# V as one level of Strassen, half swaps on ScalarE, and a new order of residuals and weights in the feed-forward, in a decoder layer on eight cores

## The chip, the cores and the metric

One Trainium2 chip, all 8 cores: two dies (cores 0 to 3 and 4 to 7), and four pairs of neighbours (0/1, 2/3, 4/5, 6/7). Each core computes 2048 of the 16384 tokens, and K and V also of the 2048 tokens before its own. The metric is the device time of the slowest core in microseconds (us). TensorE is called PE here, VectorE DVE, ScalarE ACT, GpSimd POOL, SyncE SP. The fast runs of one kernel can agree closely, but some executions fall into a slower state in which a die is granted a lower clock (a run of `b_same` took 3204.8 us with cores 0 to 3 at 0.863 to 0.873 and cores 4 to 7 at 0.990 to 0.992); only fast runs are compared below. A ratio is the mean time of one kernel's fast runs over that of the other's of the same rounds, so it is not quite the ratio of the medians that are quoted.

## The reference, cut to what matters

```python
proj = x @ w_in + b_in          # Q, K, V of two groups of heads
# group A: 8 heads of 128, three dilated windows; group B: 16 query heads of 64 on 2 K/V heads, window 128
# both: rotary positions on q and k; RMSNorm per group; concatenation -> w_out
x = layer_norm(alpha * x + mixer(x))
x = layer_norm(alpha * x + swiglu(x))      # D_MODEL 2048, D_FF 5632
```

The stages of a core follow each other: V and K (tiles of 512 tokens, 8 tiles), queries and attention, out-projection with the first LayerNorm, feed-forward in four groups (two strips of tokens, st, by two halves of the hidden units, g), the last LayerNorm.

## The kernel before

The feed-forward is already Strassen; V is plain. For tile t and block blk of 128 tokens, V is 16 products a bank, and rope of a K head is four DVE instructions:

```python
def v_tile(t, blk):                      # before
    groups = [(0, 512), (512, 1024)] if (t < 4 and not (t == 3 and blk == 3)) else [(0, 384), (384, 768), (768, 1152)]
    ...
            for kc in range(KC):         # KC = 16
                nc.tensor.matmul(bank(k, bk)[:, 0:c1 - c0], x[:, kc, blk * 128:blk * 128 + 128], wv[:, kc, c0:c1], ...)

# rope_a: t2[0:64]   = (ps[64:128] + bias) * sin      DVE
#         t2[64:128] = (ps[0:64]  + bias) * sin       DVE
#         t1         = (ps + bias) * cos              DVE
#         dst        = t1 + t2                        DVE, fp32 in, bf16 out

# ra: two rope tables, loaded two tiles ahead; KO: three buffers from which K heads are stored

for t in range(2, 8):                    # before, shortened
    if t >= 3: kb_tile(t)
    for blk in range(4): v_tile(t, blk)
    if t == 7: phase2_loads(k)           # what attention needs first
    for h in range(8): k_tile(t, h)      # each ends in a store from KO, issued by SP
    if t + 2 < 8: load_ra(t + 2)
```

`phase2_loads` issues on SP, among others, one load that reads what V's stores have written, and so waits for all of them:

```python
S_.dma("sp", k.vB, k.vs_d[TOK - 128:2 * TOK, 1024:1152]..., k.bvs, [k.bvB], "vB")
```

In the feed-forward each group is 22 up steps (`fl`, a 1 MB weight tile each, three places) and 8 down pairs (`p`, a 1.4 MB weight tile each, three places that overlap those of the up tiles). The residual rows of a down pair (`xq`) are loaded one pair ahead, the results stored to z2s:

```python
U_OFF = [WB, WB + 8192, WB + 16384]                                          # up step i uses U_OFF[i % 3]
D_OFF = [WB + (24576, 13312, 0)[i] for i in (0, 1, 2, 0, 1, 2, 1, 0)]        # place of the weights of down pair p
...
for p in range(5 if last else KC // 2):
    nxq = load_xq(p + 1) if p < 7 else None
    ...
    P("5", BB, True, True, cs);  P("2", BC, True, True, cs)
    acc(q11, BB, ALU.subtract, True);  acc(q22, BB, ALU.subtract, True)      # DVE: needs the residuals
    if p: d_sums(st, g, p, "R")                                              # DVE: needs the weights of pair p
    P("4", BA, True, True, cs);  acc(q21, BC, ALU.add, True)
    if p < 7: d_sums(st, g, p + 1, "P")                                      # DVE: needs the weights of pair p + 1
    ...
    if st == 0 and g == 1 and 1 <= p <= 4: load_x1((B11, B22, B12, B21)[p - 1])
```

The softmax here doesn't subtract the row's maximum and nothing guards it: scores larger than these inputs give would overflow.

Of the kernel before, what the change touches and what calls it, by code (L numbers as in the profile page):

```python
# [18 lines left out]
KC = D // 128  # L19
# [293 lines left out]
def persist(k):  # L313
# [12 lines left out]
    k.p_end = P.o  # L326
# [9 lines left out]
XO = 4096  # L336
X_SLOT = 16384


def rope_a(k, bk, ch, cs, sn, brope, t1, bt1, t2, bt2, dst, bdst, order=None, later=None):  # L340
# [18 lines left out]
    if later is None:  # L359
        for f in (f1, f2, f3, f4):  # L360
            f()
    else:
        later += [f1, f2, f3, f4]


def rope_b(k, bk, ch, n, cs, sn, brope, pre, bpre, t1, bt1, t2, bt2, dst, bdst, later):
# [4 lines left out]

    def tail():
        S_.pe(lambda: nc.tensor.matmul(ps, k.perm, pre[:, 0:n], start=True, stop=True), [bpre, k.bperm], [k.bBK[bk]])
        S_.dve(lambda: nc.vector.tensor_tensor(out=t1[:, 0:n], in0=pre[:, 0:n], in1=cs, op=ALU.mult), [bpre, brope], [bt1])
        S_.dve(lambda: nc.vector.tensor_tensor(out=t2[:, 0:n], in0=ps, in1=sn, op=ALU.mult), [k.bBK[bk], brope], [bt2])  # L375
        S_.dve(lambda: nc.vector.tensor_tensor(out=dst, in0=t1[:, 0:n], in1=t2[:, 0:n], op=ALU.add), [bt1, bt2], [bdst])
    later.append(tail)


def phase1(k):  # L380
    nc, S_ = k.nc, k.S
    xs = [view(k, XO + i * X_SLOT, KC * 512).rearrange("p (a b) -> p a b", a=KC) for i in range(5)]
    P = Place(k, XO + 5 * X_SLOT, 2 * ARENA_EL)
    wv, _ = P("wv", KC * VW)
    o = XO + 5 * X_SLOT
# [9 lines left out]
    ra, bra, rb, brb = [], [], [], []  # L395
    for i in range(2):
        v, b = P("ra%d" % i, 1024, F32)
        ra.append(v.rearrange("p (a b) -> p a b", a=2))
        bra.append(b)
    v, b = P("rb", 1024, F32)  # L400
    rbt, brbt = v.rearrange("p (a b) -> p a b", a=2), b
    bv, bbv = P("bv", VW, F32)
    T1 = [P("t1%d" % i, 512, F32) for i in range(2)]
    T2 = [P("t2%d" % i, 512, F32) for i in range(2)]
    PRE = P("pre", 512)
    KO = [P("ko%d" % i, 512) for i in range(3)]
    VO = [P("vo%d" % i, VW) for i in range(2)]
# [7 lines left out]
    slot_of = [0, 1, 2, 4, 0, 1, 2, 3]  # L415
# [55 lines left out]
    def v_tile(t, blk):  # L471
        x = xs[slot_of[t]]
        groups = [(0, 512), (512, 1024)] if (t < 4 and not (t == 3 and blk == 3)) else [(0, 384), (384, 768), (768, 1152)]
        banks = []
        for (c0, c1) in groups:
            bk = nx("bk", 8)
            banks.append(bk)

            def mm(bk=bk, c0=c0, c1=c1):
                for kc in range(KC):  # L480
                    ins = nc.tensor.matmul(bank(k, bk)[:, 0:c1 - c0], x[:, kc, blk * 128:blk * 128 + 128], wv[:, kc, c0:c1],  # L481
                                           start=(kc == 0), stop=(kc == KC - 1))
                return ins
            S_.pe(mm, bx[t] + bwv + ([bwvb] if c1 > 1024 else []), [k.bBK[bk]])
        v_out(t, blk, groups, banks)

    def k_tile(t, h):
        x = xs[slot_of[t]]
        bk = nx("bk", 8)
        ri = t % 2  # L490
# [8 lines left out]
        ko, bko = KO[ki := nx("ko", 3)]  # L499
        rope_a(k, bk, h, ra[ri][:, 0, :], ra[ri][:, 1, :], bra[ri], T1[ti][0], T1[ti][1], T2[ti][0], T2[ti][1], ko, bko)  # L500
# [4 lines left out]
    def kb_tile(t):  # L505
# [12 lines left out]
        ki = nx("ko", 3)  # L518
        ko, bko = KO[ki]
        rope_b(k, bk, 8, n, rbt[:, 0, 0:n], rbt[:, 1, 0:n], brbt, PRE[0], PRE[1], T1[ti][0], T1[ti][1], T2[ti][0], T2[ti][1],  # L520
# [8 lines left out]
    def load_ra(t):  # L529
        S_.dma("sp", ra[t % 2], k.ropeA_d[t], [], [bra[t % 2]], "ra%d" % (t % 2))  # L530
# [25 lines left out]
    load_ra(1)  # L556
    for h in range(8):
        k_tile(0, h)
    load_x(2, (8, 8))
    load_ra(2)  # L560
    for h in range(8):
        k_tile(1, h)
        if h == 0:
            load_x(3, (8, 8))
    load_ra(3)
    S_.dma("sp", rbt[:, :, 0:128], k.ropeBh_d, [], [brbt], "rb")
    for t in range(2, 8):
        if t == 2:
            load_x(4, (8, 8))
            load_x(5, (8, 8))  # L570
        if t == 3:
            load_x(6, (8, 8))
            load_x(7, (8, 8))
        if t >= 3:
            kb_tile(t)
        for blk in range(4):
            v_tile(t, blk)
            flush()
        if t == 7:
            k.xs, k.bx = xs, bx  # L580
            phase2_loads(k)
        if 3 <= t < 7:
            S_.dma("sp", rbt, k.ropeB_d[t - 3], [], [brbt], "rb")
        for h in range(8):
            k_tile(t, h)
        if t + 2 < 8:
            load_ra(t + 2)
    flush()
# [35 lines left out]
def phase2(k):  # L624
# [93 lines left out]
    peq = []  # L718

# [8 lines left out]
    def proj(tau, bk=None, mid=None):  # L728
# [21 lines left out]
        if ci < 8:  # L750
            pre, bpre = PRE[ti]
            rope_b(k, bk, 17 + ci, 512, rb[:, tt, 0], rb[:, tt, 1], brb, pre, bpre, T1[ti][0], T1[ti][1], T2[ti][0],
                   T2[ti][1], q[:, tt * 512:(tt + 1) * 512], bq[tt], peq)
# [149 lines left out]
    def a_banks(u):  # L903
        return (6, 7) if u >= 26 and u % 2 else (OB, LB)
# [109 lines left out]
    for tau in range(LEAD):  # L1014
        proj(tau, (6, 7, 4, 5)[tau % 4])
        if tau:
            run(peq, 1)
        if tau == LEAD - 2:
            pend = b_S(0, 0)
    for u in range(32):  # L1020
        j, kq = u // 4, u % 4
        nxt = b_S((u + 1) // 4, (u + 1) % 4) if u < 31 else None
        if u == 31:
            spend = [a_S(0, 0, 2, 0), a_S(0, 0, 1, 1)]
        b_PV(j, kq, pend)
        b_evac(j, kq)
        proj(u + LEAD, mid=lambda: run(peq, 1))
        run(dveq, 4)
        if u == 3:
# [9 lines left out]
    for u in range(32):  # L1039
# [5 lines left out]
        for p_ in range(3):  # L1045
# [4 lines left out]
            if p_ == 0:  # L1050
                run(dveq, 2 if u < 26 else 4)
# [36 lines left out]
D_OFF = [WB + (24576, 13312, 0)[i] for i in (0, 1, 2, 0, 1, 2, 1, 0)]  # L1088
# [44 lines left out]
def out_loads(k):  # L1133
# [5 lines left out]
    for st in range(2):  # L1139
        for g in range(2):  # L1140
            if st == 0 and g == 0:
                k.wlist.append(("gate", st, g))
            k.wlist += [(("u", st, f), k.wup_d[f].rearrange("q p n -> p q n"), KC * 256, KC, BF16, U_OFF[f % FG % 3]) for f in range(g * FG, (g + 1) * FG)]
# [6 lines left out]
    for c in KCB + KCA[:7]:  # L1150
        y_load(k, 1, c)

# [59 lines left out]
def phase3(k):  # L1212
# [112 lines left out]
    def load_x1(b):  # L1325
# [656 lines left out]
```

## Time and profile before

| | before |
|---|---|
| time, median of 3 runs | 2954.8 us (2952.95; the third, 3379.08, was slow) |
| span of the profiled execution, slowest core | 2858.0 us, granted clock 0.990 |
| PE busy in it | 2754.1 us (96%) |
| V and K, first to last K product | 417.4 us |
| feed-forward, first to last product start (eight cores) | 1640.7 to 1655.5 us |

A line of the time line reads: start, duration, engine, line of the program, operation, output and input with their shape, how many; in brackets the idle time just before and what ended it. Lines of the kernel before and after have different numbers. Those that are needed: feed-forward products L1399 before, L1505 after; accumulations L1745 before, L1861 after; K products L494 before, L590 after; V units L528 after; query projections L742 before, L836 after.

### The profile page before, as it was taken

Reading aid. Unit: us, or ns where it says so; the run is one execution under the profiler, and the core shown is the slowest. Engines: PE = TensorE matmul, PEld = TensorE weight load, DVE = VectorE, ACT = ScalarE, POOL = GpSimd, SP = SyncE. Lnnn points to the kernel's source line nnn. Section 1 sums busy time; section 2 is a strip of 40 time slices with the busy share of each in tenths; the row PEclk is TensorE's granted clock in tenths of the full one; section 3 lists DMA queues with packets and bytes.
Section 4 is the critical chain, followed back from the end, with each engine's and each line's share of the span. In section 5 each row is a group of like instructions: output and inputs, shape, how many; then the busy total and the mean of one; then the engine's idle time right before and its main releaser. Section 6 shows DMA issues by size and latency. Waiting matters only on the chain.

```text
span 2858.0 us, 41512 instructions; the slowest of 8 cores (2846.2 to 2858.0 us)
## 1 busy us (share of the span) xinstructions
PE 2754.1 (96%) x15081; PEld 1319.9 (46%) x15081; DVE 1933.6 (68%) x2707; ACT 736.6 (26%) x1078; POOL 562.8 (20%) x569
## 2 busy tenths in 40 slices
PE   6999999999999999999998999988999999999996
PEld 2445555444666444444443444433444444444442
DVE  0654555788788826788865666655888765666667
ACT  0000000576666327333200122111333200212115
POOL 4000000122111567411100000045200000000165
PEclk9999999999999999999999999999999999999998
DMA  9975213668666769799999755699788799555763
GB/s 156 183 138 111 62 52 87 114 98 134 152 138 167 215 144 239 140 151 151 148 159 184 138 89 87 96 199 200 155 175 172 123 196 175 103 89 89 148 133 118
DMA packets 250810, 400.58 MB, mean 140 GB/s; under 512 B 89072, under 2 KB 127088, under 8 KB 249840
## 3 DMA queue, kind: packets, MB, share of 16 engines
q0 software_dynamic: 94272, 186.43, 45.6%
q1 hardware_dynamic: 141936, 182.12, 23.5%
q10 hardware_dynamic: 14400, 29.37, 3.2%
q8 instruction: 122, 2.00, 0.3%
q14 instruction: 80, 0.66, 0.1%
HBM read 491.42 MB, written 97.06 MB: 206 GB/s over the span
## 4 chain that ended last, share of the span: by engine, by line
PE 84%; DMA 7%; DVE 3%; issue 3%; ACT 3%; POOL 1%; DVEq 0%; ACTq 0%; SPq 0%; POOLq 0%
PE sp L1399 49%; PE sp L494 8%; PE sp L1206 8%; PE sp L481 6%; PE sp L742 6%; DMA arena<-wdn 2%; DMA z2s<-arena 1%; DMA arena<-wv 1%; DMA arena<-x1s 1%; DMA arena<-z2s 1%; PE sp L550 1%; ACT arena L791 1%; DVE arena L1745 1%; POOL arena L140 1%; PE sp L514 1%
## 5 line engine op out<-in xcount | busy, mean ns | idle before, releaser
L1399 PE MATMUL sp<-arena 128*128 128x512 f16 x7408 | 1611.0, 380 | 35.7 <-DVE arena L1745 29.8
L1399 PEld LDWEIGHTS sp<-arena 128*128 128x128 f16 (+1 forms) x7408 | 725.3, 98 | 921.7 <-issue 58.0
L1662 DVE TENSOR_TENSOR arena<-sp,arena 128x512 f32<-128x512 f32 (+1 forms) x348 | 236.5, 688 | 160.7 <-PE sp L1399 145.3
L1745 DVE TENSOR_TENSOR arena<-arena,sp 128x512 f32<-128x512 f32 x257 | 167.8, 682 | 135.9 <-PE sp L1399 122.7
L742 PE MATMUL sp<-arena 128*128 128x512 bf16 x1024 | 237.0, 380 | 3.8 <-DVE arena L375 1.5
L1206 PE MATMUL sp<-arena 128*128 128x512 bf16 x1024 | 221.8, 379 | 1.0 <-DVE arena L1195 1.0
L494 PE MATMUL sp<-arena 128*128 128x512 bf16 x1024 | 222.2, 379 | 0.0
L140 POOL DMA_DIRECT2D arena<-wup x88 | 65.7, 747 | 782.1 <-DVE arena L1412 501.0
L463 DVE TENSOR_TENSOR arena<-sp,arena 128x384 bf16<-128x384 f32 (+1 forms) x81 | 48.1, 605 | 203.0 <-PE sp L481 120.0
L481 PE MATMUL sp<-arena 128*128 128x384 bf16 (+1 forms) x1040 | 182.6, 337 | 0.0
L1412 DVE TENSOR_TENSOR arena<-arena 128x2048 f16<-128x2048 bf16 (+1 forms) x118 | 158.9, 1347 | 30.7 <-DMA arena<-wdn 30.7
L1249 POOL TENSOR_TENSOR arena<-arena 128x512 f32<-128x512 f32 x117 | 150.3, 1285 | 145.1 <-DVE arena L1745 107.5
L1696 ACT ACTIVATE arena<-sp 128x512 f32<-128x512 f32 x86 | 51.4, 597 | 436.4 <-PE sp L1399 436.4
L1420 DVE TENSOR_TENSOR arena<-arena 128x2048 f16<-128x2048 bf16 (+1 forms) x118 | 159.3, 1350 | 0.0
L1251 POOL TENSOR_TENSOR arena<-arena 128x512 f32<-128x512 f32 x117 | 156.7, 1340 | 10.4 <-ACT arena L1248 8.0
L1206 PEld LDWEIGHTS sp<-arena 128*128 128x128 bf16 x1024 | 100.0, 98 | 122.9 <-issue 3.2
L1662 DVE TENSOR_TENSOR arena<-arena 128x512 f16<-128x512 f32 (+1 forms) x304 | 155.0, 568 | 2.4 <-DMA x1h<-arena 2.4
L494 PEld LDWEIGHTS sp<-arena 128*128 128x128 bf16 x1024 | 100.2, 98 | 120.3
L369 ACT ACTIVATE arena<-sp,arena 128x512 bf16<-128x512 f32 (+1 forms) x37 | 24.7, 666 | 506.1 <-PE sp L514 430.8
L1248 ACT ACTIVATE arena<-arena 128x512 f32<-128x512 f32 x117 | 73.7, 630 | 311.2 <-DVE arena L1745 160.4
L742 PEld LDWEIGHTS sp<-arena 128*128 128x128 bf16 x1024 | 95.9, 98 | 123.2 <-issue 14.8
L481 PEld LDWEIGHTS sp<-arena 128*128 128x128 bf16 x1040 | 101.7, 98 | 79.6
(145 smaller groups left out, 2493.1 us busy)
## 6 DMA issues: line engine op xcount, KB each, us to landing
arena<-wup POOLq DMA_DIRECT2D x88, 1024.0 KB, 10.8
arena<-wdn POOLq DMA_DIRECT2D x32, 1408.0 KB, 19.0
z2s<-arena SPq DMA_DIRECT2D x48, 512.0 KB, 11.9
arena<-wob SPq DMA_DIRECT2D x32, 512.0 KB, 7.2
arena<-xres SPq DMA_DIRECT2D x32, 512.0 KB, 8.7
x1s<-arena ACTq DMA_DIRECT2D x64, 256.0 KB, 8.8
arena<-x1s SPq DMA_DIRECT2D x32, 512.0 KB, 13.5
arena<-z2s SPq DMA_DIRECT2D x32, 512.0 KB, 15.6
```

What stands on the lines that cost most here:

```text
L140: i = self._add(q, lambda: eng.dma_start(out=out, in_=in_), reads, writes, joins, semkey=semkey)
L481: ins = nc.tensor.matmul(bank(k, bk)[:, 0:c1 - c0], x[:, kc, blk * 128:blk * 128 + 128], wv[:, kc, c0:c1], start=(kc == 0), stop=(kc == KC ...
L494: ins = nc.tensor.matmul(bank(k, bk), wk[h][:, kc, :], x[:, kc, :], start=(kc == 0), stop=(kc == KC - 1))
L742: ins = nc.tensor.matmul(bank(k, bk), w[:, kc, :], x[:, kc, :], start=(kc == 0), stop=(kc == KC - 1))
L1206: ins = nc.tensor.matmul(bank(k, bk), w[:, kc, :], y[:, kc, hh * 512:(hh + 1) * 512], start=(first and i == 0), stop=(last and i == len(kc ...
L1249: S_.pool(lambda: nc.gpsimd.tensor_tensor(out=za, in0=za, in1=z, op=ALU.add), [bz, bza], [bza])
L1251: ss["pend"] = [lambda: S_.pool(lambda: nc.gpsimd.tensor_tensor(out=qa, in0=qa, in1=sq, op=ALU.add), [bsq, bqa], [bqa])]
L1399: ins = nc.tensor.matmul(bank(k, bk), w, x, start=(first and i == 0), stop=(last and i == len(ws) - 1), skip_group_check=True)
L1412: S_.dve(lambda: nc.vector.tensor_tensor(out=v, in0=w[:, 0:n, :], in1=w[:, n:2 * n, :], op=ALU.add), [bw], [b])
L1420: S_.dve(lambda: nc.vector.tensor_tensor(out=v, in0=w[:, :, 0:128], in1=w[:, :, 128:256], op=ALU.subtract), [bw], [b])
L1662: S_.dve(lambda: nc.vector.tensor_tensor(out=o, in0=a, in1=b, op=op), [ba, bb], [bo])
L1745: S_.dve(lambda: nc.vector.tensor_tensor(out=v, in0=v, in1=o, op=op), [b, bo], [b])
```

## The change

The intent: 112 products for V where there were 128 (a seventh product saved in every eight), room for it won by giving up a rope table and a K store buffer, less work for DVE in rope, and a feed-forward in which residuals and weights come earlier. The core of the diff, with cuts:

```diff
@@ V and K @@
-    xs = [... for i in range(5)]
+    xs = [... for i in range(4)]
-    for i in range(2):
-        v, b = P("ra%d" % i, 1024, F32)          # two rope tables
+    v, bra = P("ra", 1024, F32)                  # one
-    KO = [P("ko%d" % i, 512) for i in range(3)]
+    KO = [P("ko%d" % i, 512) for i in range(2)]
+    G = [P("g%d" % i, 8 * 512, F16) for i in range(3)]     # sums of w_v
+    xp, bxp = P("xp", 8 * 512, F16)                        # sums of x: P, Q, R
+    xq, bxq = P("xq", 8 * 256, F16)
+    xr, bxr = P("xr", 16 * 256, F16)
+    VB = P("vb", 512)                                      # group B's V, stored apart
...
+    def v_unit(t, i):                            # 7 products of 8 matmuls for 2 x 128 tokens x 1024 columns
...
     for h in range(8):
         k_tile(0, h)
+        if 1 <= h <= 5:
+            w_sum(h - 1)
+    load_ra(1)
+    for t in range(1, 8):
+        if t >= 2:
+            v_unit(t, 0)
...
+            v_unit(t, 1)
+            flush()
+            load_ra(t)
+            if t >= 3:
+                vb_tile(t)
         if t == 7:
             phase2_loads(k)
         for h in range(8):
             k_tile(t, h)
+            if h in (1, 3, 5) and t < 7:
+                x_sum(t + 1, h // 2)
@@ rope of K @@
+    if swap:
+        for i, j in ((0, 64), (64, 0)):
+            S_.act(lambda i=i, j=j: nc.scalar.activation(out=t2[i:i + 64], in_=ps[j:j + 64], func=AF.Identity, ...
@@ attention @@
+        run(t1q, 1)                              # DVE: rope product t1 of group B, ahead of b_evac
         b_PV(j, kq, pend)
         b_evac(j, kq)
-        proj(u + LEAD, mid=lambda: run(peq, 1))
         run(dveq, 4)
+        proj(u + LEAD, mid=(lambda: run(peq, 1)) if u < 31 else first_a)
@@ feed-forward @@
-D_OFF = [WB + (24576, 13312, 0)[i] for i in (0, 1, 2, 0, 1, 2, 1, 0)]
+D_OFF = [WB + (24576, 13312, 0)[p % 3] for p in range(8)]
+def u_off(st, f):
+    i = f % FG
+    if st + f // FG == 0:
+        return U_OFF[i % 3]
+    return U_OFF[0] if i == 0 else WB + 24576 if i == 1 else U_OFF[(i - 1) % 3]
...
+            def ring(n):                         # six places for residual rows, fetched two pairs ahead
+                e = (3, 4, 0, 2, 1, 5)[n % 6]
...
-                    if 1 <= p <= 4:
-                        load_x1((B11, B22, B12, B21)[p - 1])
+                    for i in {6: (6, 7), 7: ()}.get(p, (p,)):
+                        load_x1(i)               # half as large, one a pair
```

## The prediction

Passages that state rules of the hardware which no trace shows are cut from the text, and each cut is marked. The sum: -20.7 + 13 - 4 - 27 = -39 us, shaded to -37, so 2918 us. 2816 bf16 elements took 0.575 ns each on DVE and 512 fp32 elements 1.33; from the first, 2.4 us for a sum of 4096 was the author's estimate. K stores issued from 90 to 146 us, where the DMA share was 1.11, landed after 6.9 to 11.8 us, those from 200 to 500 after 1.9 in the median. And on DVE the accumulations (L1745, 1966.26 us) start only after the sum L1412, which had waited 10.92 us for its weights.

> **What bounds the kernel now.** I read the cores first: all eight lie within 0.5% at a granted clock of about 0.99, so core 7 speaks for all. The profiled span is 2858.0 us and the timed median 2954.8 us; I carry differences of the span over one to one. Then the busy table and the table of stretches:
>
> ```profile
> PE 2754.1 (96%) x15081; PEld 1319.9 (46%) x15081; DVE 1933.6 (68%) x2707; ACT 736.6 (26%) x1078; POOL 562.8 (20%) x569
> ...
> 84.00:139.00 55.00, 55.00 (x257) 24.95 (x255) 43.07 (x59) 0.00 (x0) 1.77 (x2) 1.00 1.11 180
> 139.00:202.00 63.00, 63.00 (x307) 29.04 (x304) 36.07 (x51) 0.37 (x1) 5.26 (x6) 1.00 0.78 133
> ...
> 680.00:712.00 32.00, 27.12 (x243) 15.51 (x244) 29.55 (x40) 18.92 (x25) 8.26 (x9) 0.95 0.61 103
> ...
> 910.00:945.00 35.00, 28.72 (x389) 21.40 (x387) 28.76 (x45) 25.13 (x35) 9.19 (x6) 0.95 0.86 240
> ...
> 1450.00:1580.00 130.00, 120.25 (x555) 53.65 (x553) 73.06 (x94) 0.00 (x0) 5.91 (x8) 1.00 0.94 183
> ...
> 1860.00:1990.00 130.00, 113.49 (x503) 49.79 (x501) 73.58 (x89) 16.39 (x26) 67.35 (x56) 0.93 0.96 200
> ```
>
> After the window come its length and the busy time of PE, weight load, DVE, ACT and POOL, then clock, DMA share and GB/s. TensorE is the bound: it idles 104 us in all (2858.0 - 2754.1). About 25 of these are the first loads, 27 the tail after the last product. From 84 to 501 us, where K and V of tiles 0 to 7 are made, it does not idle at all. So Strassen pays there in full, unless it creates a new wait. The idle time that order changes can reach lies in five places: 4.9 us at 680, 6.3 at 910, 9.8 at 1450, 16.5 at 1860, and 4.2 at 2287 with some 5 more near 2692 and 2781.
>
> What these gaps are, the time lines of PE and DVE tell (start, duration, instruction, idle before it):
>
> ```profile
> 1506.66 2.53 PE L1399 MATMUL sp<-arena 128*128 128x512 f16 x11 [2.30 <-DVE arena L1743]
> ...
> 1920.94 37.80 PE L1399 MATMUL sp<-arena 128*128 128x512 f16 x165 [7.01 <-DVE arena L1745]
> 1967.08 3.15 PE L1399 MATMUL sp<-arena 128*128 128x512 f16 x7 [8.34 <-DVE arena L1745]
> ...
> 1505.82 0.69 DVE L1743 SCALAR_TENSOR_TENSOR arena<-arena,sp 128x512 f32<-128x512 f32 x1 [6.10 <-DMA arena<-x1s]
> ...
> 1920.11 0.69 DVE L1745 TENSOR_TENSOR arena<-arena,sp 128x512 f32<-128x512 f32 x1 [7.85 <-DMA arena<-z2s]
> ...
> 1964.71 1.63 DVE L1412 TENSOR_TENSOR arena<-arena 128x2816 f16<-128x2816 bf16 x1 [10.92 <-DMA arena<-wdn]
> ```
>
> DVE is named, but DVE itself stands at a load: the residual pair (x1s or z2s) or the weight tile of the next down pair. [...]the accumulations that free the banks stand behind.
>
> [...]in the chain, 128 products of 512 columns take 27.63 us (215.9 ns each), 48 of 384 take 7.80 (162.5), and 16 of 128 take 0.89 (55.6):
>
> ```profile
> 138.84 27.63 PE sp L481 x128
> ...
> 194.09 0.89 PE sp L514 x16
> ...
> 254.64 7.80 PE sp L481 x48
> ```
>
> [...]Here 2816 bf16 elements take 1.62 us (0.575 ns each) and 512 fp32 take 0.68 (1.33 ns)[...]. [...]
>
> **The change part by part.**
>
> V, products. Before: tile 2 is 128 products of 512 columns, 27.63 us; tile 3 is 96 of 512 and 48 of 384, 28.52; tiles 4 to 7 are 192 of 384 each, 31.20. Sum 27.63 + 28.52 + 4 x 31.20 = 180.95 us. After: each tile is two units of 7 products of 8 matmuls, 112 x 215.9 = 24.18 us, six tiles 145.1; the 128 columns of group B go separately, 16 + 4 x 64 = 272 matmuls x 55.6 = 15.1. Sum 160.2. **Saved: 20.7 us.**
>
> V and K on DVE. Rope by the two half swaps costs DVE about 3 x 0.75 + 0.69 = 2.95 us a head now; afterwards one 0.75, one fp32 product 0.69 and one sum 0.69, about 2.2 with gaps. ScalarE takes two half copies of about 0.6 us each; it does 3 us of work from 84 to 501 us, so it is free. Per tile: 8 x 2.2 + sums of x 2.4 + 1.2 + 2.4 + two units of nine 0.69 operations (12.4) + some 3 for group B = 39 us against a tile of 24.2 + 3.6 + 27.6 + 3.5 = 59 us of PE. In the steady state (tiles 3 to 7) DVE is not the bound.
>
> V, start. This is the dear place. The fp16 sums come from space: the rope table goes from two buffers to one, the buffer of K stores from three to two, and x gets four slots. Loads keep the engines full until 146 us (x of tile 3: issued at 32.8, landed 113.5 us later). Followed by hand with the trace's durations: heads of tile 0 run on DVE from 92.3 on with five sums of w_v (2.4 each) between them and K stores landing 7 to 11 us after issue, so that two buffers give a head every 4 to 5 us; head 7 ends near 129. Only then can the one rope table be reloaded, and loads of it took 10 to 12 us here, so DVE starts tile 1 near 140 where PE has nearly finished tile 1 (138.9). After that, at two heads per store landing: sum P of tile 2 at 147, Q at 154, R at 163, head 7 at 168. PE is then held before products 5, 1, 3 and 7 of the first unit: it ends near 172 rather than 151. That is a wait of 21 us. Each term rests on a landing time that the new traffic may shorten, the table's above all, so I charge 13.
>
> ```profile
> DMA to landing us min/median/max: 6.9/7.7/11.8
> ```
>
> (That is for the K stores issued between 90 and 146 us.)
>
> Attention. The rope product t1 is drawn ahead and group A's rotation is left for the next step rather than standing in DVE's queue before the masks; the first scores of group A come in the middle of the last projection. It can take part of 1.5 (six waits of 0.25 us for L375), 4.9 and 6.3 us. The later change of banks (from step 28 rather than 26) gives a little back. I count 4.
>
> Feed-forward. (a) At pair 0 product 2 is now completed first and 6 follows, so nothing waits for the first two accumulations: 0.96 + 0.20 us, four times, 4.6. (b) Residual pairs are fetched two pairs ahead in a ring of six: a pair is 77 x 0.2159 = 16.6 us, a store lands in 12 to 13 and a load in 14 to 18; before, both had to fit into one pair and 4.8 us, now into about two. It removes 2.30 + 1.73 (1500) and 7.01 (1920), perhaps 0.52 (2342): 11. (c) The weights of pair 6 go where pair 3 was rather than 4, one pair earlier: 2.90 + 1.66, 8.34, 2.48, 2.44, 17.8 together. (d) In three of four groups the weight tile of pair 1 can now start only when the last up tile is done, one step of 12 us later. It lands (19.0 us median) when pair 0 has some 2 us left; I charge 4 for the three. Its sum: 4.6 + 11 + 17.8 - 4 = 29, less 2 because some late loads will remain: 27.
>
> Total: -20.7 + 13 - 4 - 27 = -39 us by this account, and I shade it to -37 for what I overlooked: **2918 us**.
>
> **The rivals.** One: the wait at tile 2 is as long as followed, 21 us, and eats all of Strassen's gain; the feed-forward repair alone remains, 2954.8 - 31 = 2924. For it speaks that every term was taken from a measured duration; against it, that the new program asks for fewer rope tables in the congested time and x sums need x only at 130 us, when it has landed. Two: no wait forms and all reachable gaps close: 20.7 + 8 + 33 = 62, 2893. Against it: products lie between DVE steps with little slack at each group's start. Three: the ring trades one late load for another, since in these stretches DMA already shows 0.94 to 0.96 busy: pair 1's weights come late in three groups by 5 us each, and prefetched residuals push the weights back. Then the feed-forward gives 12, and with a full wait at tile 2 the time is 2940. Four: DVE, now with about 7 us more work a tile in V and K, becomes the bound there. I computed 39 of 59 us, so only bunching could do that.
>
> **Range and chances.** The limits are the second and the third rival, little of each: 2898 to 2940. Faster by over 2% means under 2895.7, a gain of 59 us or all that can be had: 0.06. Slower by over 2% needs waits of some 110 us more than counted: 0.01. The rest is within 2%.
>
> **What would show it.** From 84 to 501 us before: the same work should end some 5 to 15 us earlier, with PE idle between 139 and 172 us only, before the first Strassen unit, DVE waiting there for the rope table and for K stores. Later V tiles should take 24.2 us plus 3.6 and show no idle PE. The waits of L1743 and L1745 on x1s and z2s, and those of the weight sums on wdn for pairs 6 and 7, should be nearly gone; a new wait on wdn may show at pair 1 of the last three groups. I would be wrong if PE idles at every V tile, if the wait at tile 2 is absent, or if the gaps at 1500 and 1920 stay.

## The result, and the profile after

The changed kernel ran at 2955.5 us (fast runs 2951.8 to 2956.2), the kernel before beside it at 2943.5 to 2954.8: ratio 0.9999 with a 95% interval of 0.9975 to 1.0023. The change moved nothing, and 2955.5 lies outside the range of 2898 to 2940.

**First the clock, or the profiles mislead.** ("The first chip" below is the one of this comparison; the profile of before may be from another.) These are lines of the page of the kernel after: the span, the busy table, the granted clock in 40 slices, and the group of the feed-forward products (count, busy us, mean ns, idle us before them):

```profile
span 2950.7 us, 41710 instructions; the slowest of 8 cores (2914.8 to 2950.7 us)
PE 2850.0 (97%) x14985; PEld 1327.9 (45%) x14985; DVE 1944.5 (66%) x2714; ACT 833.6 (28%) x1218; POOL 566.3 (19%) x569
...
PEclk9989999999999999988999999989989999998888
...
L1505 PE MATMUL sp<-arena 128*128 128x512 f16 x7408 | 1719.0, 399 | 7.4 <-DVE arena L1861 5.1
```

The same lines of the page of the kernel before:

```profile
span 2858.0 us, 41512 instructions; the slowest of 8 cores (2846.2 to 2858.0 us)
...
PEclk9999999999999999999999999999999999999998
...
L1399 PE MATMUL sp<-arena 128*128 128x512 f16 x7408 | 1611.0, 380 | 35.7 <-DVE arena L1745 29.8
```

The same 7408 products took 399 ns after and 380 before, because the profile after was taken at a granted clock of 0.946 and that of before at 0.990. So the two spans say nothing of each other. The clock records of the traces show the form that this took: core 1 of the profile after has 44 stretches of 15.2 us at 13/16 of the full clock (0.8125), 670 us in all, from the second half of the out-projection on; on the eight cores there are 44 to 94 of 15.2 us and less, 4.1 us or more apart; the profile of before has none. These are the "pulses" of the expectations below. What can be read is the idle time: 35.7 us before the feed-forward products became 7.4. PE has 96 products fewer and yet the time is the same. Either the clock takes back what the change gives, or PE waits elsewhere.

**The waits at tile 2.** The time line of PE after, core 1. K of tile 1 should give way to V of tile 2 at 138 us:

```profile
137.88 1.89 PE L528 MATMUL sp<-arena 128*128 128x512 f16 x8
142.65 1.89 PE L528 MATMUL sp<-arena 128*128 128x512 bf16 x8 [2.89 <-DVE arena L508]
149.54 6.48 PE L528 MATMUL sp<-arena 128*128 128x512 f16 x16 [5.00 <-DVE arena L508]
163.10 20.34 PE L528 MATMUL sp<-arena 128*128 128x512 f16 x80 [7.08 <-ACT arena L542]
...
508.25 9.78 PE L836 MATMUL sp<-arena 128*128 128x512 bf16 x32 [7.37 <-DVE arena L355]
```

Three waits, 15.0 us, on the sums of x (L508) and on a copy (L542) that itself waits until the last rope sum of a K head on DVE (L358) has freed the buffer that the copy writes. The products after them are slow too: 16 take 6.48 us where 16 x 0.216 = 3.5 are due, 80 take 20.34 rather than 17.3. The clock of the window shows why (the third number from the end; the columns are those of the prediction's table):

```profile
138.00:184.00 46.00, 31.03 (x117) 12.32 (x115) 29.65 (x41) 9.41 (x14) 1.76 (x2) 0.81 0.68 120
```

The clock records of the same execution stand at 0.5 for 6.8 and for 10.2 us in this place, with 3.4 us at full clock between them, and at full clock for over 130 us on both sides. So 15.0 us of idle cost 21: the chain of the same execution puts the end of the second unit at 183.4, which is 45.3 us after 138.1, for 24.2 us of work. From there on the units are what the prediction said (start, duration, line, count):

```profile
183.44 27.63 PE sp L590 x128
211.07 12.09 PE sp L528 x56
223.16 0.89 PE sp L610 x16
224.05 12.09 PE sp L528 x56
...
292.55 3.57 PE sp L570 x64
```

and no wait follows in V and K. The 508.25 line of the time line above is a second place, which the prediction didn't have: 7.4 us of idle before the first query projection, and 32 products at 9.78 rather than 6.9 us after it; the clock from 500 to 520 us was 0.74, with a record of 10.2 us at 0.5.

The reasons must therefore be sought in four places: the clock, the start of tile 2, the entry into attention, and the feed-forward, where the idle time on the slowest core fell and yet the time did not.

### The profile page after: what moved, and what is told of

It reads as the page before. It is cut to its first block, busy times and chain, and to the rows that moved or that the text cites. A ratio compares the mean times of both kernels' runs of the same rounds, so it can differ in the third digit from the quotient of the medians.

```text
span 2950.7 us, 41710 instructions; the slowest of 8 cores (2914.8 to 2950.7 us)
## 1 busy us (share of the span) xinstructions
PE 2850.0 (97%) x14985; PEld 1327.9 (45%) x14985; DVE 1944.5 (66%) x2714; ACT 833.6 (28%) x1218; POOL 566.3 (19%) x569
## 3 DMA queue, kind: packets, MB, share of 16 engines
q1 hardware_dynamic: 145920, 182.12, 20.7%
## 4 chain that ended last, share of the span: by engine, by line
PE 83%; DMA 7%; DVE 4%; ACT 3%; issue 2%; POOL 1%; DVEq 0%; SPq 0%; ACTq 0%; POOLq 0%
PE sp L1505 56%; PE sp L1311 8%; PE sp L528 5%; PE sp L590 5%; PE sp L836 4%; DMA ka<-arena 2%; DMA vs<-arena 2%; ACT arena L885 2%; DMA arena<-wdn 1%; DMA arena<-wv 1%; DVE arena L945 1%; DMA z2s<-arena 1%; POOL arena L140 1%; PE sp L610 0%; PE sp L966 0%
## 5 line engine op out<-in xcount | busy, mean ns | idle before, releaser
L1505 PE MATMUL sp<-arena 128*128 128x512 f16 x7408 | 1719.0, 399 | 7.4 <-DVE arena L1861 5.1
L1505 PEld LDWEIGHTS sp<-arena 128*128 128x128 f16 (+1 forms) x7408 | 752.4, 102 | 974.3 <-issue 392.7
L1861 DVE TENSOR_TENSOR arena<-arena,sp 128x512 f32<-128x512 f32 x257 | 169.9, 684 | 175.6 <-PE sp L1505 175.4
L1812 ACT ACTIVATE arena<-sp 128x512 f32<-128x512 f32 x86 | 51.4, 598 | 457.0 <-PE sp L1505 457.0
L362 ACT ACTIVATE arena<-sp,arena 64x512 f32<-64x512 f32 x128 | 87.5, 684 | 308.9 <-PE sp L590 238.3
L528 PE MATMUL sp<-arena 128*128 128x512 f16 (+1 forms) x672 | 153.1, 389 | 15.0 <-DVE arena L508 7.9
L1311 PEld LDWEIGHTS sp<-arena 128*128 128x128 bf16 x1024 | 100.7, 98 | 125.0 <-issue 11.9
L836 PEld LDWEIGHTS sp<-arena 128*128 128x128 bf16 x1024 | 96.1, 98 | 130.3 <-issue 23.4
L590 PEld LDWEIGHTS sp<-arena 128*128 128x128 bf16 x1024 | 100.0, 98 | 119.7
L1775 ACT ACTIVATE arena<-sp 128x512 f32<-128x512 f32 x90 | 53.6, 598 | 308.4 <-PE sp L1505 298.6
L1778 DVE TENSOR_TENSOR arena<-arena,sp 128x512 f32<-128x512 f32 x86 | 59.1, 688 | 91.7 <-PE sp L1505 91.3
## 6 DMA issues: line engine op xcount, KB each, us to landing
z2s<-arena SPq DMA_DIRECT2D x42, 512.0 KB, 11.8
```

Source lines behind the costliest of these rows:

```text
L528: ins = nc.tensor.matmul(bank(k, bk), w[:, c, :], m[:, c, :], start=(first and c == 0), stop=(last and c == 7), skip_group_check=True)
L590: ins = nc.tensor.matmul(bank(k, bk), wk[h][:, kc, :], x[:, kc, :], start=(kc == 0), stop=(kc == KC - 1))
L836: ins = nc.tensor.matmul(bank(k, bk), w[:, kc, :], x[:, kc, :], start=(kc == 0), stop=(kc == KC - 1))
L1311: ins = nc.tensor.matmul(bank(k, bk), w[:, kc, :], y[:, kc, hh * 512:(hh + 1) * 512], start=(first and i == 0), stop=(last and i == len(kc ...
L1505: ins = nc.tensor.matmul(bank(k, bk), w, x, start=(first and i == 0), stop=(last and i == len(ws) - 1), skip_group_check=True)
L1778: S_.dve(lambda: nc.vector.tensor_tensor(out=o, in0=a, in1=b, op=op), [ba, bb], [bo])
```

## The experiments

The theories, as the expectations use them: **W**, that the waits named above explain the loss and can be taken away (with it the question which of them; **S** adds that their terms simply add up); **C**, that a lower granted clock gives back what PE saves (0.946 in the profile after, 0.990 in that of before) - that something, "the limiter", lowers it when PE waits less is the author's conjecture and shown by no run; and later **U** (called D in the expectations) and **X** for the feed-forward, told there. In every run whose label begins with z the weights of the out-projection and of the feed-forward are zero, a wrong result: the instructions and transfers are the same, the data that PE multiplies is not. All 14 runs were made on chips 15, 13, 5 and 1; numbers are compared within a chip unless said otherwise.

```diff
# every z run, in the preparation of the inputs
-    w_out = np.asarray(w_out, f)[0]
-    w_up = np.asarray(w_up, f)[0]
-    w_down = np.asarray(w_down, f)[0]
+    w_out = np.zeros(np.asarray(w_out).shape[1:], f)
+    w_up = np.zeros(np.asarray(w_up).shape[1:], f)
+    w_down = np.zeros(np.asarray(w_down).shape[1:], f)
```

### Is it the clock? Both kernels as they are, and both with zero weights

`b_same` and `a_same` are the two kernels without an edit; `z_before` and `z_after` have only the zero weights. From two of the expectations a reason is cut that no run shows: from that of `b_same` why C would lower the clock, from that of `z_before` why zeros would take the pulses away. What is left of the latter names two outcomes: without pulses a clock of 0.99 and 2840 to 2865 us, and, if they don't depend on the data, 2950.

> The kernel before, unchanged, to see the granted clock of its ordinary runs (its profiled run had 0.990 and 2858 us where its timed ones took 2953 us). Theory C (the limiter took the gain[...]): about 2950 us at a mean clock of 0.955 or more, clearly above that of the changed kernel (0.947 to 0.955). Theory W (new waits took the gain, the clock is the same): 2950 us and a mean clock equal to the changed kernel's within 0.002. If its clock is 0.99 at 2950 us both are wrong.

> The changed kernel, unchanged, on the same chip. Both theories: 2950 to 2956 us, within 0.3% of the kernel before. Theory C: mean clock lower than in the kernel before by about 0.005 to 0.01, since some 20 us less idle at one time need a lower clock. Theory W: the same mean clock.

> The kernel before with the output, up and down weights set to zero (a wrong result on purpose): the same instructions[...]. [...]clock about 0.99 and 2840 to 2865 us, as in the one undisturbed profile. If they do not depend on the data: 2950 us.

> The changed kernel with the same zero weights. Theory C: without pulses the schedule's own gain shows: 29 us less idle in the feed-forward, 7 to 11 us more in the first 950 us, so 15 to 22 us under the run with zero weights of the kernel before. Theory W: no difference (within 5 us).

Measured on chip 15, all at profiled clocks of 0.977 to 0.993:

| run | fast runs, us | ratio to before [95%] |
|---|---|---|
| b_same | 2853.0, 2855.1, 2884.2, 2885.4 | 1.0032 [0.9956, 1.0109] |
| a_same | 2853.5, 2853.6, 2856.5, 2857.2, 2866.5, 2870.7 | 0.9979 [0.9931, 1.0027] |
| z_before | 2852.2 to 2859.8 (six) | 0.9965 [0.9920, 1.0009] |
| z_after | 2848.3, 2849.4, 2849.5, 2857.1, 2874.2 | 0.9965 [0.9910, 1.0021] |

Both kernels lie 100 us lower than on the first chip, at a clock of 0.99 rather than 0.95, and they are still equal, with real data and with zeros. So C is not needed: where no lower clock is granted, the change gains nothing either. That doesn't exclude C for the first chip itself. Nor do these runs show whether the pulses depend on the data, since in the fast ones the clocks with real data (0.975 to 0.993) were as high as with zeros (0.977 to 0.993). What varies between the runs of before (2853 or 2884) goes with one or two pairs of cores at about 0.98. Two later profiles caught such cores: 6 and 7 of `z_after` at 0.977 and 0.980, where the other cores had 0.987 to 0.991, and 0 to 3 of `z_fix2` at 0.980 to 0.984, where the others had 0.989 to 0.994. From here on the zero-weight runs are used, which were disturbed less often on this chip.

The spans of the cores tell more than the times. `z_after`, cores 0 to 5 (6 and 7 were disturbed in this execution, at 0.977 and 0.980):

```profile
core 0: 2818.2 us, clock 0.991
core 1: 2849.2 us, clock 0.987
core 2: 2817.3 us, clock 0.991
core 3: 2843.1 us, clock 0.987
core 4: 2848.6 us, clock 0.987
core 5: 2816.0 us, clock 0.991
```

In `z_before` they lie between 2842 and 2854. So half of the cores did gain, some 31 us (the median of the eight was 2849, the fast cores have 2817), and the time is that of the other half: in each pair one core is fast and one slow. That 31 is near the predicted 37 is luck, as the fast cores gained nearly all of it in the feed-forward (30 us on core 0). The stages of core 1 in the two runs, from the first product of one to the first of the next:

| stage, core 1 | z_before | z_after | difference |
|---|---|---|---|
| first K product starts | 83.0 | 85.6 | +2.6 (first loads, varies by run) |
| first to last K product | 417.4 | 415.9 | -1.5 |
| last K product to first query projection | 0.2 | 6.8 | +6.6 |
| first query projection to first out-projection | 440.1 | 442.5 | +2.4 |
| out-projection | 230.3 | 230.3 | 0 |
| feed-forward, first to last product | 1649.9 | 1636.8 | -13.1 |
| after that, to the end | 31.5 | 31.3 | -0.2 |
| sum | 2852.4 | 2849.2 | -3.2 |

In core 0 of `z_after` the feed-forward took 1612.1, against 1641.9 in core 0 of `z_before`.

### Which part? V and K alone, the feed-forward alone

`z_v_only` is the kernel before with the V and K part of the diff alone; `z_ff_only` with the feed-forward part alone, and the constant that it uses:

```diff
# z_v_only: @@ V and K @@ and @@ rope of K @@ of the diff above, nothing of @@ attention @@ and @@ feed-forward @@
# z_ff_only: @@ feed-forward @@ of the diff above, and
 XO = 4096
+FREE = 2048
```

> Only the V and K part of the change (Strassen, rope swap, one rope table, two K store buffers), attention and feed-forward as before; weights of the last two thirds zero. Theory S (the terms are additive: the first stage keeps 2 us of 20.7, its entry into attention costs 5 to 7): V and K end 2 us earlier, first projection waits 5 to 7 us, attention itself 438 to 439 us as before, 2858 us in all. Rival (the entry wait and the 3 us of attention come from the reordering there): no entry wait, 2853 us.

> Only the feed-forward part of the change (rings, prefetch, order of pair 0). Theory S with pairs of cores that compete for loads: in each pair (0 and 1, 2 and 3, ...) the core that enters the feed-forward later gains about 10 us, the other about 33; slowest core 2844 to 2848, fastest near 2822. Rival (the late core loses only because the new first stage spreads the cores): all eight gain about 30, slowest core 2825.

`z_v_only`: 2861.3, 2864.6, 2864.8 us, ratio 1.0014 [0.9997, 1.0031] on chip 13. Strassen alone brought nothing or cost a little: cores 0 and 2 have 416.1 and 418.4 us from the first to the last K product, then 6.6 and 7.6 us before the first projection. Attention, in the old order here, took 439.2 to 441.2, against a median of 439.1 in `z_before` and 440.9 to 442.5 in `z_after`. So the new order of attention brought none of its 4 us; it may have cost one. In `z_after`, core 1, there are 23 small waits (5.5 us in all) of group B's products with V for the evacuation of their bank, ahead of which DVE now does t1; cores 0 and 1 of `z_v_only`, in the old order, have three such waits.

`z_ff_only`: 2850.8 to 2851.3 us, ratio 0.9970 [0.9954, 0.9987]. It has the split as well, without any of the V part, so the split belongs to the feed-forward. It isn't wholly new: in `z_before` and `b_same` the feed-forward of the two cores of a pair differs by 6 to 10 us, here by 18 to 34. Cores 0 to 3:

```profile
core 0: 2845.7 us, clock 0.990
core 1: 2811.8 us, clock 0.995
core 2: 2813.8 us, clock 0.994
core 3: 2839.6 us, clock 0.990
```

The time line of PE on core 0 shows where the slow core of a pair loses; core 1 has no wait over 1.8 us in the same stage:

```profile
1586.15 289.34 PE L1408 MATMUL sp<-arena 128*128 128x512 f16 x1332 [3.11 <-ACT arena L1717]
1883.70 66.00 PE L1408 MATMUL sp<-arena 128*128 128x512 f16 x297 [8.21 <-DVE arena L1764]
...
2303.85 113.12 PE L1408 MATMUL sp<-arena 128*128 128x512 f16 x516 [3.81 <-DVE arena L1764]
```

DVE on core 0, just before: the first sum of the weights of down pair 2 (L1421) waits 11 us for those weights, and the accumulations (L1764) that free the banks stand behind it. The same sum for pair 1, at 1859.86, had waited 1.7 us:

```profile
1869.55 0.68 DVE L1764 TENSOR_TENSOR arena<-arena,sp 128x512 f32<-128x512 f32 x1
1881.33 1.63 DVE L1421 TENSOR_TENSOR arena<-arena 128x2816 f16<-128x2816 bf16 x1 [11.11 <-DMA arena<-wdn]
1882.88 1.88 DVE L1764 TENSOR_TENSOR arena<-arena,sp 128x512 f32<-128x512 f32 x3
```

The requests for the weights of pairs 1 and 2 in this group (st 0, g 1; the time line of POOL), first in `z_before`, core 1, then in `z_ff_only`, core 0:

```profile
1838.14 0.74 POOL L140 DMA_DIRECT2D arena<-wdn  x1 [22.70 <-DVE arena L1412]
1850.23 0.74 POOL L140 DMA_DIRECT2D arena<-wdn  x1 [11.35 <-DVE arena L1412]
```

```profile
1844.26 1.48 POOL L140 DMA_DIRECT2D arena<-wdn  x2 [34.78 <-DVE arena L1421]
```

Two requests 12 us apart have become two in one go. In `z_before`, core 1, each landed within 13.8 us. Landing times of the two (requests from 1825 to 1852 us) in `z_ff_only`, core 0:

```profile
DMA to landing us min/median/max: 15.5/25.9/36.2
```

core 1:

```profile
DMA to landing us min/median/max: 11.0/17.9/24.8
```

And the window 1846 to 1876 (the last two numbers are the DMA share and GB/s), core 0 and then core 1:

```profile
1846.00:1876.00 30.00, 29.49 (x137) 13.21 (x135) 18.51 (x26) 3.08 (x5) 7.08 (x6) 1.00 0.97 174
```

```profile
1846.00:1876.00 30.00, 30.00 (x141) 13.61 (x140) 19.68 (x27) 5.01 (x8) 16.85 (x15) 1.00 1.04 233
```

Both cores' transfer engines are full (0.97 and 1.04), but one core moves 233 GB/s and the other 174. In all 16 pairs of `z_after`, `z_ff_only`, `z_fix1` and `z_fix2` the loser was the core of the pair that had entered the feed-forward later; here core 0 entered at 1172.0 and core 1 at 1168.8. So pairs, not dies, are the unit here. Together the two cores moved 407 GB/s in this window; what it is that they share, these runs don't show.

### Take away the waits of V and K

The new kernel has one rope table, so that of tile 1 can only be loaded when tile 0 no longer needs it. `z_fix1` is `z_after` with two repairs: a second rope table in the place of xr, which is not yet needed at that time, and a third K store buffer that it shares with group B's V.

```diff
+    o_xr = P.o                                   # rope table of tile 1 lives where xr will be
+    ra1 = view(k, o_xr, 1024, F32)...
+    S_.dma("sp", ra1, k.ropeA_d[1], [], [bra1], "ra1")      # ahead of the heads of tile 0
     ...
-    load_ra(1)
+    load_ra(2)                                   # and x_sum(2, 2), which writes xr, after the last head of tile 1
     VB = P("vb", 512)
+    KO.append(VB)
```

> The whole change, and in it a second rope table for tile 1 (in the space of sum R, which is then made after the last head of tile 1) and a third buffer for K stores (the one of group B's V). Theory: the wait of TensorE at tile 2 (17 to 20 us in the changed kernel) comes from these two; it falls to under 6 us, V and K end 12 to 15 us earlier, 2838 to 2845 us. Rival (the x loads or the vector engine's amount of work set it): it stays above 12 us.

Measured on chip 13: 2837.2, 2837.6, 2838.3 us, ratio 0.9923 [0.9907, 0.9940]. First to last K product is now 396.6 to 403.7 us on the eight cores, 398.7 in the median: 13.7 to 20.8 of the 20.7 us arrive. The time line of PE on core 0 keeps one wait at tile 2, and the clock of the window stays at 1.00:

```profile
150.44 15.70 PE L532 MATMUL sp<-arena 128*128 128x512 f16 x72 [1.90 <-DVE arena L542]
```

```profile
138.00:184.00 46.00, 44.10 (x205) 19.82 (x204) 31.39 (x45) 9.83 (x15) 1.75 (x2) 1.00 0.82 140
```

Against `z_ff_only` the time fell by 13 us rather than 18; the entry into attention, which this run keeps, accounts for 5.4 of it (5.6 us from the last K product to the first projection, before 0.2).

What DVE waited for in `z_after`, core 1, says why both repairs were needed:

```profile
137.94 0.75 DVE L355 SCALAR_TENSOR_TENSOR arena<-sp,arena 128x512 f32<-128x512 f32 x1 [9.33 <-DMA arena<-ropeA]
...
147.97 0.69 DVE L358 TENSOR_TENSOR arena<-arena 128x512 bf16<-128x512 f32 x1 [2.23 <-DMA ka<-arena]
...
156.65 0.69 DVE L358 TENSOR_TENSOR arena<-arena 128x512 bf16<-128x512 f32 x1 [3.47 <-DMA ka<-arena]
...
504.58 0.69 DVE L358 TENSOR_TENSOR arena<-arena 128x512 bf16<-128x512 f32 x1 [12.10 <-DMA ka<-arena]
```

The table (ropeA) is one wait of 9.3 us; after it every second head waits for a store of K heads (ka).

### The entry into attention

The last of those lines is the entry: DVE stands 12.1 us for a K store. The chain of `z_after` on core 1 in this stretch holds two transfers in a row:

```profile
475.83 17.79 DMA vs<-arena
...
494.27 10.22 DMA ka<-arena
```

and SP's queue shows what lies between them (us in total, times, longest):

```profile
SPq L206 <- DMA vs<-arena: 9.2, 1, 9.2
```

The load of group B's V waits on SP for the last V store (vs), which was issued only just before and lands in 17.8 us among the new loads; the K stores are issued on SP too and stand behind it. In `z_before`, core 1, SP doesn't wait for a V store at all in this stretch, and the wait of DVE for a K store is short:

```profile
DVE arena L357 <- DMA ka<-arena: 4.4, 1, 4.4
```

`z_fix2` moves that one load to where attention starts, on top of the two repairs, and takes the old order in attention:

```diff
 # phase2_loads
-    S_.dma("sp", k.vB, k.vs_d[...], k.bvs, [k.bvB], "vB")
 # start of the attention stage
+    k.S.dma("sp", k.vB, k.vs_d[...], k.bvs, [k.bvB], "vB")
     load_kB(k, 1)
```

> As the one before, and the load of group B's V for attention is queued after the last K stores rather than before them, and attention is in its old order. Theory: the entry wait of 5 to 8 us goes because K stores no longer stand behind that load, and attention returns to 438.6 from 441 to 442 us: 8 to 10 us less than the run before, 2830 to 2836. Rival (the entry wait comes from the loads' bandwidth): 3 us less only.

Measured: one undisturbed run, 2824.0 us; two that count as fast but had a die at 0.98, 2855.3 and 2856.2; the ratio, 0.9950 [0.9891, 1.0008], settles nothing. The profile does for this stage: on core 4, at a clock of 0.994, the wait at the entry is 1.8 us, and 31 products take 7.07 us, so the slow products (32 in 9.78 us in the profile after) are gone too (from the last K product to the first projection cores 4 to 7 take 0.4 to 3.5 us):

```profile
483.26 7.07 PE L844 MATMUL sp<-arena 128*128 128x512 bf16 x31 [1.76 <-DVE arena L355]
```

In this run attention took 437.2 to 440.7 us on undisturbed cores, in the old order.

### The split in the feed-forward: U against X

Two parts of the change add traffic where the slow core loses. **U**: with the new `u_off` the last up step lies in the third place, over the room of the weights of down pair 1; so those can only be requested when the last up step is done, and they start together with the weights of pair 2, residuals and x1. Pair 1 is served first (15.5 us to landing on core 0 of `z_ff_only`); what comes late is pair 2 (36.2 us). **X**: the loads of x1 now come at every pair. `z_ff_u` and `z_ff_x1` are `z_ff_only` with one of them taken back:

```diff
 # z_ff_u: the last up step uses the first place again, the second to last the third
-    return U_OFF[0] if i == 0 else WB + 24576 if i == 1 else U_OFF[(i - 1) % 3]
+    return WB + 24576 if i == 1 else U_OFF[i % 3]
 # z_ff_x1: x1 in pairs 1 to 4, as before
-                    for i in {6: (6, 7), 7: ()}.get(p, (p,)):
+                    for i in (2 * p - 2, 2 * p - 1) if 1 <= p <= 4 else ():
```

> The feed-forward part alone (as z_ff_only, zero weights), with one difference: the up tiles are placed so that the room of pair 1's down weights comes free one up step (12 us) earlier, as in the kernel before. Theory D (the later core of a pair loses because the change starts the down weights of pairs 1 and 2 together, at the last up step, and they then land after up to 36 us): the gaps at pair 1 (7.9 us at 1870, some 3 at 2300) go, the later cores gain 8 to 12 us, slowest core 2838 to 2842. Rival X (the earlier loads of the next stage's x crowd them out): no change, 2849 to 2851.

> The feed-forward part alone, with the loads of the next stage's x at pairs 1 to 4, a block each, as in the kernel before, and not from pair 0 on in halves. Theory X: the gap at pair 1 near 1870 goes and the slowest core gains 5 to 10 us, 2840 to 2845. Theory D: gap at pair 1 stays, 2849 to 2852; perhaps the wait for x at the stage's start changes by 1 to 3 us.

Chip 5. There the kernel before ran at 2883 to 2892 us, which is its disturbed level, so the ratios to it (0.9806 and 0.9845) are not used; the z runs are compared with each other and with `z_ff_only`.

`z_ff_u`: 2824.9 to 2831.6 us, mean 2828.5, where `z_ff_only` had 2851.0 on chip 13: 22.5 less, more than was expected of U, though across two chips. The split is nearly back to what it was before the change (4 to 10 us in a pair), cores 0 to 3:

```profile
core 0: 2814.1 us, clock 0.994
core 1: 2822.5 us, clock 0.993
core 2: 2816.7 us, clock 0.993
core 3: 2823.6 us, clock 0.992
```

The requests for pairs 1 and 2 are 12.1 us apart again and land in at most 11.8 us on core 0 and 14.1 on core 1. The feed-forward takes 1609.4 to 1620.8 us on all eight cores.

`z_ff_x1`: 2838.4, 2840.9, 2843.6 us, 10 less than `z_ff_only` on the other chip, but the split stays: 2837.7 and 2812.5 on cores 0 and 1, feed-forward 1637.5 and 1613.1, down weights landing up to 33.3 us after their request on core 0. The feed-forward of the four slow cores took 1638.7 us on average, against 1640.5 in `z_ff_only`, so the stage itself hardly shows the 10 us. On chip 5 alone `z_ff_u` is 12.4 us faster than `z_ff_x1`. So U is the cause that the split grew; that X is a term is not shown.

### Together, and with real weights

`z_best` is `z_fix2` with U's line; `after_u` is the changed kernel with U's line alone and real weights; `best` is `z_best` with real weights; `z_ra2` is `z_after` with the second rope table but still two K store buffers, one look.

```diff
# z_best, best: the diffs of z_fix2 and of z_ff_u; after_u: that of z_ff_u; z_ra2: that of z_fix1 without
-    KO.append(VB)
```

> All of the change with the repairs together: second rope table for tile 1, third K store buffer, group B's V load after the K stores, old order in attention, up tiles placed so that pair 1's weights load early; zero weights. Theory D and the additive terms: 2824 us of the run with the first three repairs, less 8 to 10: 2812 to 2818, 1.4 to 1.6% under the kernel before. Theory X: 2822 to 2826.

> The changed kernel, real weights, with the one line on the place of the up tiles repaired. Theory D: the later cores' loss of 20 to 25 us goes, all eight cores alike, ratio to the kernel before 0.988 to 0.992 where the clock is not throttled. Rival (with real data the limiter takes the gain): 0.998 to 1.002 with a mean clock lower than the kernel before's by 0.006 or more.

> All repairs together with real weights; right result expected. Theory: 45 to 50 us under the kernel before on the same chip in undisturbed runs, ratio 0.982 to 0.985. Rival (limiter): ratio above 0.992 at a mean clock lower by 0.006 or more than that of the kernel before.

> The changed kernel with only the second rope table for tile 1 (K stores still in two buffers), zero weights. If the table is the larger part of the wait at tile 2, the wait falls from 17 to 20 us to about 5 to 8; if the K stores in two buffers are, it stays at 10 or more.

| run | chip | fast runs, us | ratio to before [95%] | correct |
|---|---|---|---|---|
| z_best | 5 | 2806.9, 2807.4, 2809.2, 2812.1 | not used (before at its disturbed level) | no |
| after_u | 1 | 2834.0, 2840.0, 2842.1, 2845.8 | 0.9903 [0.9848, 0.9958] | yes |
| best | 1 | 2811.2, 2814.3, 2815.0, 2815.9 | 0.9804 [0.9758, 0.9849] | yes |

`best` beats both kernels, at clocks of 0.990 to 0.996, where the fast runs of before (2859.5 to 2885.3) had 0.979 to 0.993: more work per time did not bring a lower clock, which speaks against C once more. Against the four runs of before that no core disturbed (2859.5 to 2862.5) it is 47 us faster. Core 6 of `z_best`, its slowest, has 401.3 us from the first to the last K product (before 417.4), 2.7 before the first projection, 438.6 in attention, 1618.6 in the feed-forward. In `after_u` the feed-forward takes 1612.0 to 1622.2 us on the eight cores (in `a_same`, on chip 15, 1611.4 to 1645.6): U's repair holds with real weights.

`z_ra2` ran at 2849.8 us. The time line of PE on core 0:

```profile
146.05 6.35 PE L531 MATMUL sp<-arena 128*128 128x512 f16 x16 [4.25 <-DVE arena L511]
159.92 3.57 PE L531 MATMUL sp<-arena 128*128 128x512 f16 x8 [7.52 <-ACT arena L545]
164.16 16.24 PE L531 MATMUL sp<-arena 128*128 128x512 f16 x72 [0.67 <-DVE arena L541]
```

Waits of 12.4 us here, 11.3 and 14.7 on cores 1 and 4, against 14.3 and 12.9 on cores 0 and 1 of `a_same` and 15.6 on core 1 of `z_after`; with both repairs 1.7 to 2.9. So the early table alone removes little, though DVE waited longest for it: the stores then take its place. The third buffer is needed. Whether it would do alone was not run and stays open.

## Why the prediction was wrong, by its own steps

| step | predicted | measured on the slow core of a pair | verdict |
|---|---|---|---|
| V, products | -20.7 | units 12.09 us each as counted; 13.7 to 20.8 gained when the waits are away | right |
| V, start at tile 2 | +13 | +19.4 (`z_after`, core 1) to +21.1 (after, core 1) | mis-sized |
| DVE in the steady state | no bound | no wait from tile 3 on | right |
| entry into attention | not there | +6.6 | missed |
| attention, order | -4 | about +1, and some +1 from the slow products after the entry (an estimate; 32 took 9.61 us on core 1 of `z_after`) | wrong |
| feed-forward (a), (b), (c) | -33.4 | -34 on the fast core of a pair (1612 against a median of 1646) | right |
| feed-forward (d) | +4, and 2 left over | 20 to 26 more on the slow core than on the fast one (1632 to 1638 on undisturbed cores), so -8 to -14 in all | mis-sized |

**V's start is a term of the sum that was mis-sized, against its own working.** The prediction followed the heads by hand and got 21 us, then charged 13 because "each rests on a landing time that the new traffic may shorten". It did not: the table took 9.9 us (10 to 12 were assumed), K stores 7.2 us at the median. The first rival had the right number. That is partly luck: the idle time itself was 15.0 us, six less than counted, and the half clock (0.81 on average from 138 to 184 us), which the count lacked, made 21.1 of it.

**The entry was not in the account at all.** The prediction counted two K store buffers as a cost at tile 2 only. At tile 7 the same two buffers meet a V store that the change puts later, a load that waits for it on SP, and K stores behind that load. Moving the one load, with the two repairs, left 1.8 us of the wait.

**Attention** had reckoned waits of single instructions as removable. Some were: on core 1 the six for L375 (1.5 us) are gone, and those of the products at L947, now L1041, fell from 5.1 to 3.6. But t1 ahead of the evacuation made 23 others of 0.24 us each (5.5 us on core 1 of `z_after`), and 3.8 us before L1015 and 3.0 before later projections are new or longer.

**The feed-forward: (d) failed as the step, though (a) to (c) were right.** It followed the weights of pair 1 alone: requested when the last up step is done, landing after the median of 19.0 us, a cost of 4 for three groups. For pair 1 that was not far off (15.5 us to landing, 1.7 of wait on core 0 of `z_ff_only`). What it left out is that the weights of pair 2 are now requested in the same moment; on the core of the pair that comes later these took 36.2 us and held DVE for 11.1. The time is that of the slowest core, and each pair has one. The third rival was nearest: it named the crowding, though at pair 1, 5 us in each group and a gain of 12 in all; 8 to 14 were measured. One line that lets the room go free one up step earlier (`z_ff_u`) took the feed-forward of the slow cores from 1636 to 1647 us down to 1617 to 1621.

Summed for the slow core: -1.5 for V and K, +6.6, +2.4, -13.1: a gain of 6 on core 1, within the scatter of the first stage (2.6 there) and of the cores (2842 to 2854 before). The prediction's own total of -39 lacks the 7 of V's start, 7 of the entry, 6 of attention and 14 to 19 of the feed-forward, and the rest is what it had right.

Of the signs that it had set itself, PE's waits in one place near 139 to 172 us and none in the later V tiles came as written. Of the waits of DVE in the feed-forward (core 1, `z_before` to `z_after`), those on x1s fell from 17.8 to 1.0 us, those on z2s only from 15.1 to 9.5. A new wait on wdn at pair 1 "may show", it said; the long one showed at pair 2. The sign that failed clearly was the first, V and K ending 5 to 15 us earlier: in `z_after` they took 0.7 to 6.8 us less on the eight cores.

Open: why the core that comes later gets the smaller share of the transfers (174 against 233 GB/s), and why the first chip granted only 0.946 to 0.957 to the kernel after in its profile where chips 15, 13, 5 and 1 granted about 0.99 to undisturbed cores. Open too is where the feed-forward's gain went on that first chip. The profile after shows the waits of V's start and of the entry there, but in the feed-forward its PE waits only 1.7 to 9.3 us and its pairs differ by only 5 to 12 us, so (d) as found on the other chips did not act there in that size. No profile of the kernel before in that state exists, so whether the clock took the gain there is neither shown nor excluded.

## What to carry to other kernels

When buffers are given up to make room, follow every wait that those buffers hid, in each stage that uses them, and charge what the hand count says rather than a part of it; idle time can cost more than its length: 15.0 us in three waits cost 21.1 here, with the clock at 0.5 for 6.8 and 10.2 us. When a weight tile may be requested only at a barrier, look what else is requested there, follow the last of these loads (36.2 us here) and not the first (15.5), and take the landing time of the core that comes last, not the median of one core. Read all cores before the slowest one: a split between neighbours that is wider than before says that a change gained on one core and lost on the other.
